# Where the gate projections stand in the state space stage, and when small matmuls of B and C are issued

## The chip, the cores and the metric

The kernel runs on one core of a Trainium2 chip. Five engines work side by side on that core and meet through semaphores: TensorE (PE, the matmuls), VectorE (DVE), ScalarE (ACT), GpSimd (POOL) and SyncE (SP), which here only issues transfers between the chip's memory and the on-chip buffers. The metric is the device time of one execution in microseconds (us). Lower is better.

## What is computed

Two layers of an encoder over 512 tokens of 1024 channels, all in float32. Each layer projects its input once into three branches: a bidirectional state space branch (SSD), differential attention, and cross-attention into 256 memory tokens. Sigmoid gates merge the three, an output projection and a layer norm close the layer. The change lies in the SSD branch and in the gates. Cut to that:

```python
proj = jnp.einsum('bsd,de->bse', x, w_in[layer])
z, xbc, dt_raw, dq, dk, dv, dg, cq, cg, gl = jnp.split(proj, splits, axis=-1)
xbc = jax.nn.silu(_centred_dwconv(xbc, conv_w, conv_b))       # x (32 heads of 64), B and C (4 groups of 128)
# one direction of the chunked scan: 4 chunks of 128 tokens, 4 groups of 8 heads
a_cum = jnp.cumsum(a, axis=-1)
seg = a_cum[..., :, None] - a_cum[..., None, :]
decay = jnp.exp(jnp.where(lower, seg, -jnp.inf))
y_diag = jnp.einsum('bcqgn,bcsgn,bgrcqs,bcsgrp->bcqgrp', cm, bm, decay, xs)
decay_states = jnp.exp(a_cum[..., -1:] - a_cum)
states = jnp.einsum('bcqgn,bgrcq,bcqgrp->bcgrpn', bm, decay_states, xs)
# prev: the states carried from chunk to chunk
y_off = jnp.einsum('bcqgn,bcgrpn,bgrcq->bcqgrp', cm, prev, jnp.exp(a_cum))
# both directions are summed, then
y = y.reshape(Bsz, L, SSD_INNER) * jax.nn.silu(z.astype(jnp.float32))
y_ssd = _rmsnorm(y, norm_w)
gates = jax.nn.sigmoid(gl.reshape(Bsz, S, N_BRANCH, D_MODEL) + gate_b[layer])
merged = gates[:, :, 0] * (y_ssd @ w_br_ssd) + gates[:, :, 1] * (...) + gates[:, :, 2] * (...)
```

## The kernel before

**Units.** Almost all of TensorE's work comes in units: one tile of 128x1024 weights is loaded (`wr`), ScalarE rounds it to `wh`, VectorE computes the rest `wl`, and TensorE makes 24 matmuls of 128x512 from the three products wl*xh, wh*xl, wh*xh into one bank `pj`. Such a unit is called a whole unit below, and its 24 matmuls wide ones. `emit` walks a list of steps, `self.plan`, filled by `self.T(fn, unit)`: a step with a unit gets its weights, loaded and split some steps ahead.

**The SSD stage** (`ssd`) runs once per layer, over 4 groups g of 8 heads. In each group come the units B (`bpart`), C (`cpart`), X0 to X3 (`xpart`: the projection of 128 channels of x, then a convolution on ScalarE and VectorE, `conv`), with the output units W of the group before between them, and in the first group the small DT unit and its tables (`dt_tables`) after X0. Then come `states`, and four times a unit Z (`zpart`) and a block Y (`ypart`). In the trace's names: `bC` and `cC` are B and C after their convolution, `bT` is B transposed on TensorE through the bank `pt`; `gs` is the product of B and C, which `cpart` makes in a bank `pm`; `xsC` is a block of x and `xsT` its transposition; `cum` are the cumulative sums of the decay, which go through ScalarE (`eb`) to the chip's memory (`dab`) and come back, spread over 128 partitions, as `ab`.

**States.** `states` multiplies `xsT` with weights into `xw` on VectorE, and TensorE multiplies `xw` with `bT`, six times: these small matmuls read `xw,bT` in the trace. Every `xw` reads all four blocks of `xsT`.

**Blocks.** `ypart(g, b)` handles two heads. For each it loads `ab` (two buffers, `bufs=2`), takes the minimum with a mask and later the sum and the product with `gs` on VectorE, with eight exponentials on ScalarE between; the product is `m` (three buffers). The eight small matmuls `m,xsT` of the block need both heads' `m`. A new `ab` is loaded when a buffer comes free, which is when the `m` of an earlier head is done.

**Gates.** `AHEAD` says after which block of which group the projection of which gate is made in advance: `(0, 1): [(2, 0)]` puts the gate of branch 2, tile 0, after block (0, 1). Such a unit (`gate_ahead`) is a whole unit whose tanh, `tg`, is stored to memory (`dgt`) and read back later. Nothing near it needs its result, so it is TensorE work that can stand in any place. GATE20 below is the unit of gate (2, 0), and so on.

**Order.** The tile framework has a scheduler that arranges each engine's instructions from the program's order and priorities; on the chip every engine then takes its list in that fixed order. `self.late(n)` lowers the priority of what stands in it by n, so that the scheduler lets work that comes later in the program go first:

```python
    def late(self, n):

        return self.tc.high_priority(offset=-n)
```

`xpart` uses it for its transpositions with LX = 70, `bpart` and `cpart` don't. At the end of the stage, `norm` sums the squares `sqa` (gathered on GpSimd) with four tiny matmuls and makes the scale `rB`, which `fin` needs; `gpart` are the gates of this branch itself, G00 to G07 below.

Of the kernel before, what the change touches and what calls it, by code (L numbers as in the profile page):

```python
# [20 lines left out]
P = 128  # L21
# [15 lines left out]

AHEAD = {(0, 1): [(2, 0)], (0, 2): [(2, 1)], (0, 3): [(2, 2)], (1, 0): [(2, 3)], (1, 2): [(2, 4)],  # L40
         (2, 0): [(2, 5)], (2, 2): [(2, 6)], (3, 0): [(2, 7)], (3, 2): [(1, 0)]}

LX, LD, LN = 70, 80, 300
# [6 lines left out]
def bc(ap, shape):  # L52
    return ap.broadcast_to(shape)


class Net:
# [367 lines left out]
    def ssd(self, l):  # L424
# [10 lines left out]
        def bpart(g):  # L435
            def f(wh, wl):
                self.bC = self.t(self.sp, [P, S], "bC")
                self.conv(self.proj(wh, wl), 16 + g, self.bC)
                pt = self.bank(self.pt, "pt")
                for c in range(4):  # L440
                    self.tr(pt[:, c * P:(c + 1) * P], self.bC[:, c * P:(c + 1) * P])
                self.bT = self.t(self.sp, [P, S], "bT")
                self.act(self.bT, pt)
            return f

        def cpart(g):
            def f(wh, wl):
                self.cC = self.t(self.sp, [P, S], "cC", bufs=2)
                self.conv(self.proj(wh, wl), 20 + g, self.cC)
                pg = self.bank(self.pm, "pm")  # L450
                for c in range(4):
                    q = slice(c * P, (c + 1) * P)
                    self.mm(pg[:, q], self.bC[:, q], self.cC[:, q])
                self.gs = self.t(self.sp, [P, 4, P], "gs", bufs=2)
                self.act(self.gs, pg.rearrange("p (c q) -> p c q", c=4))
                self.xsT = self.t(self.sp, [P, 4, S], "xsT", bufs=2)
                self.xsC = {}
            return f

        def xpart(g, b):  # L460
            def f(wh, wl):
                xc = self.xsC[b] = self.t(self.sp, [P, S], f"xsC{b}")
                self.conv(self.proj(wh, wl), 4 * g + b, xc)
                pt = self.bank(self.pt, "pt")
                with self.late(LX):
                    for c in range(4):
                        self.tr(pt[:, c * P:(c + 1) * P], xc[:, c * P:(c + 1) * P])
                self.act(self.xsT[:, :, b * P:(b + 1) * P], pt.rearrange("p (c e) -> p c e", c=4))
            return f

        def states(g):
            def f():
                sp = self.sp
                self.prev = {}
                for d, order in ((0, (0, 1, 2)), (1, (3, 2, 1))):
                    hs = slice(d * 32 + g * 8, d * 32 + g * 8 + 8)
                    old = None
                    for c in order:
                        xw = self.t(sp, [P, 8, 64], "xw", bufs=2)
                        self.tt(xw, self.xsT[:, c, :].rearrange("p (h e) -> p h e", h=8),  # L480
                                bc(self.wst[:, c, hs, None], [P, 8, 64]), ALU.mult)
                        ps = self.bank(self.pm, "pm")
                        self.mm(ps, self.bT[:, c * P:(c + 1) * P], xw)
                        pv = self.t(sp, [P, 8, 64], f"prev{d}{c}")
                        psv = ps.rearrange("p (h e) -> p h e", h=8)
                        if old is None:
                            self.act(pv, psv)
                        else:
                            self.tt(pv, old, bc(self.dtot[:, c, hs, None], [P, 8, 64]), ALU.mult)
                            self.tt(pv, pv, psv, ALU.add)  # L490
                        old = pv
                        self.prev[d, c + 1 if d == 0 else c - 1] = pv.rearrange("p h e -> p (h e)")
            return f

        def zpart(g, b):
            def f(wh, wl):
                ps = self.proj(wh, wl)
                th = self.t(self.sp, [P, S], "th", bufs=2)
                self.act(th, ps, AF.Tanh, scale=0.5)
                self.sz = self.t(self.sp, [P, S], "sz", bufs=2)  # L500
                self.stt(self.sz, th, 1.0, ps, ALU.add, ALU.mult)
            return f
# [58 lines left out]
        def wpart(g, u):  # L561
            def f(wh, wl):
                yh, yl = self.yhl[g]
                for i in range(2):
                    ps = self.bank(self.pj, "pj")
                    for k in range(4):
                        c = slice(k * 256 + i * P, k * 256 + (i + 1) * P)
                        self.mm3(ps, wh[:, c], wl[:, c], yh[:, k, :], yl[:, k, :], k == 0, k == 3)
                    o = self.br[:, 2 * u + i, :]
                    if g == 0:  # L570
                        self.act(o, ps)
                    else:
                        self.tt(o, o, ps, ALU.add)
            return f

        def keep(g):
            def f():
                self.yhl = {g: (self.yh, self.yl)}
            return f
# [16 lines left out]
        def gpart(j):  # L596
            def f(wh, wl):
                self.gt[j] = self.gate(self.sp, wh, wl, 0, j, "th" if j % 4 < 2 else "sz")
            return f
# [11 lines left out]

        ahead = AHEAD
        self.ahead_gates = {ij for v in ahead.values() for ij in v}
        self.dgt = {}
        self.T(begin)
        for g in range(4):
            jobs = [(bpart(g), (l, UB + g)), (cpart(g), (l, UC + g))]
            jobs += [(xpart(g, b), (l, UXS + 4 * g + b)) for b in range(4)]
            for i, (fn, u) in enumerate(jobs):
                self.T(fn, u)  # L620
                if g == 0 and i == 2:
                    self.T(lambda: self.dt_tables(l))
                if g and i > 1:
                    self.T(wpart(g - 1, i - 2), (l, UBS + 4 * (g - 1) + i - 2))
            self.T(states(g))
            for b in range(4):
                self.T(zpart(g, b), (l, UZ + 4 * g + b))
                self.T(ypart(g, b))
                for i, j in ahead.get((g, b), ()):
                    self.gate_ahead(l, i, j, lambda: self.sp, "tg")  # L630
            self.T(keep(g))
        self.gt = {}
        self.T(norm)
        for j in range(3):
            self.T(gpart(j), (l, UGL + j))
        for u in range(4):
            self.T(wpart(3, u), (l, UBS + 12 + u))
        for j in range(KC):
# [596 lines left out]
```

## Time and profile before

| | |
|---|---|
| time, median of 3 runs | 2219.3 us (2218.12 to 2221.23) |
| the profiled execution's own time | 2223.68 us |
| its span in the trace | 2221.9 us, granted clock 0.997 |
| TensorE busy | 2171.0 us, 98% |
| VectorE busy | 1585.9 us, 71% |
| ScalarE busy | 1004.3 us, 45% |
| SSD stage, layer 0 | from the start to some 470 us |
| SSD stage, layer 1 | some 1162 to 1625 us |

TensorE is busy nearly always, so the time is that of its matmuls and of the few places where it waits. A wait shows as idle time before an instruction, with the engine and the tile that ended it. Since matmuls are pipelined, a wait is read as what the distance of two starts has over its usual value.

### The profile page before, as it was taken

What the parts mean: (1) busy time and instruction counts of PE and PEld (TensorE: products, weight loads), DVE (VectorE), ACT (ScalarE), POOL (GpSimd) and SP (SyncE); (2) the same over time, 40 slices, a digit from 0 to 9 for tenths busy, and PEclk for the clock granted to TensorE, in tenths of its full rate; (3) what the DMA queues carried; (4) which work ended last, traced back from release to release, by engine and by line L of the source; (5) the groups of instructions that cost most, each with busy time, mean ns of one, the idle gap of its engine ahead of it and who ended that gap; (6) DMA issues with size and microseconds to landing.
All of it is one profiled execution on the core that took longest, in us unless ns stands there. A gap on an engine that the chain in (4) does not pass through costs nothing.

```text
span 2221.9 us, 29523 instructions
## 1 busy us (share of the span) xinstructions
PE 2171.0 (98%) x11330; PEld 1768.0 (80%) x11330; DVE 1585.9 (71%) x2440; ACT 1004.3 (45%) x1895; POOL 54.2 (2%) x38
## 2 busy tenths in 40 slices
PE   8999999999999999999999999999999999999998
PEld 6787877788887888878887777777788887888786
DVE  7887878758554777766467888888754547777567
ACT  5664545424442454543355564545423324554440
POOL 0000000000000000000000100000100000000000
PEclk9999999999999999999999999999999999999999
DMA  4654554425553322224564654454434333222353
GB/s 149 182 160 144 144 136 144 125 86 167 168 173 117 95 85 79 77 89 147 152 214 122 177 146 145 133 152 132 124 105 132 105 113 94 75 84 81 91 154 112
DMA packets 106162, 283.73 MB, mean 128 GB/s; under 512 B 12524, under 2 KB 13092, under 8 KB 105764
## 3 DMA queue, kind: packets, MB, share of 16 engines
q1 hardware_dynamic: 106020, 281.84, 42.4%
q8 instruction: 89, 1.46, 0.3%
q14 instruction: 53, 0.43, 0.1%
HBM read 255.55 MB, written 17.85 MB: 123 GB/s over the span
## 4 chain that ended last, share of the span: by engine, by line
PE 71%; DVE 14%; DMA 8%; ACT 5%; issue 1%; POOL 0%; SPq 0%; POOLq 0%; DVEq 0%; ACTq 0%
PE pj L103 55%; PE pm L103 13%; DMA ab<-dab 5%; DVE wl L81 3%; PE pt L111 2%; DVE ab L81 2%; DVE acc L84 2%; ACT ab L91 1%; ACT wh L91 1%; DMA wr<-wu 1%; DVE y L81 1%; DVE rx L81 1%; PE pt L103 1%; DMA fth<-rd 1%; DVE m L81 1%
## 5 line engine op out<-in xcount | busy, mean ns | idle before, releaser
L103 PE MATMUL pj<-xh,wl 128*128 128x512 f32 x1664 | 669.2, 402 | 11.0 <-DVE wl L81 8.9
L103 PE MATMUL pj<-xh,wh 128*128 128x512 f32 x1664 | 661.0, 397 | 0.0
L103 PE MATMUL pj<-xl,wh 128*128 128x512 f32 x1664 | 658.5, 396 | 0.0
L81 DVE TENSOR_TENSOR wl<-wr,wh 128x1024 fp32r<-128x1024 f32 x330 | 405.7, 1230 | 109.0 <-ACT wh L91 108.1
L91 ACT ACTIVATE wh<-wr 128x1024 fp32r<-128x1024 f32 x330 | 347.4, 1053 | 228.4 <-PE pj L103 147.4
L103 PEld LDWEIGHTS pj<-xh,wl 128*128 128x128 f32 x1664 | 313.9, 189 | 91.2 <-issue 18.3
L103 PEld LDWEIGHTS pj<-xh,wh 128*128 128x128 f32 x1664 | 313.8, 189 | 71.7 <-issue 5.7
L103 PEld LDWEIGHTS pj<-xl,wh 128*128 128x128 f32 x1664 | 314.2, 189 | 63.6 <-issue 3.6
L91 ACT ACTIVATE ab<-ab,bias 128x128 f32<-128x128 f32 x512 | 160.8, 391 | 120.5 <-DVE ab L81 119.7
L84 DVE SCALAR_TENSOR_TENSOR acc<-pj,hcw,acc 128x510 f32<-128x510 f32 x192 | 142.4, 744 | 24.2 <-ACT acc L91 22.8
L91 ACT ACTIVATE fpp<-pm,fmx 128x512 f32<-128x512 f32 x128 | 87.9, 687 | 84.3 <-DVE fmx L889 83.6
L889 DVE TENSOR_REDUCE fmx<-pm 128x1 f32<-128x512 f32 x128 | 87.0, 686 | 45.9 <-PE pm L103 45.5
L103 PE MATMUL pj<-yl,wh 128*128 128x512 f32 x256 | 102.4, 400 | 0.9 <-DVE yl L84 0.9
L103 PE MATMUL pj<-yh,wh 128*128 128x512 f32 x256 | 103.0, 403 | 0.0
L81 DVE TENSOR_TENSOR ab<-ab,cst 128x1024 f32<-128x1024 f32 x64 | 85.4, 1334 | 24.4 <-DMA ab<-dab 24.4
L103 PE MATMUL pj<-dy,wh 128*128 128x512 f32 (+1 forms) x384 | 102.2, 354 | 0.1
L103 PE MATMUL pj<-yh,wl 128*128 128x512 f32 x256 | 102.0, 399 | 0.0
L103 PE MATMUL pj<-cy,wh 128*128 128x512 f32 x256 | 78.8, 389 | 0.0
L103 PEld LDWEIGHTS pj<-dy,wh 128*128 128x128 f32 x384 | 67.8, 189 | 11.0 <-DVE dy L81 0.9
L103 PE MATMUL pj<-wh,xl 128*128 128x256 f32 x256 | 74.8, 292 | 0.0
L81 POOL TENSOR_TENSOR sqa<-sqa,sz 128x512 f32<-128x512 f32 x32 | 52.9, 1654 | 845.6 <-ACT sz L91 845.6
L103 PE MATMUL pj<-wl,xh 128*128 128x256 f32 x256 | 72.4, 283 | 0.0
(273 smaller groups left out, 3269.1 us busy)
## 6 DMA issues: line engine op xcount, KB each, us to landing
wr<-wu SPq DMA_DIRECT2D x336, 512.0 KB, 3.7
ab<-dab SPq DMA_DIRECT2D x64, 512.0 KB, 5.7
eb<-deb SPq DMA_DIRECT2D x64, 256.0 KB, 4.7
mkv<-dkv SPq DMA_DIRECT2D x16, 512.0 KB, 4.5
rsw<-rx SPq DMA_DIRECT2D x128, 64.0 KB, 2.0
dgt<-tg SPq DMA_DIRECT2D x18, 256.0 KB, 2.8
dkv<-mo SPq DMA_DIRECT2D x16, 256.0 KB, 4.2
dkv<-q SPq DMA_DIRECT2D x16, 256.0 KB, 3.6
```

Source lines behind the costliest of these rows:

```text
L81: (eng or self.nc.vector).tensor_tensor(out=out, in0=a, in1=b, op=op)
L84: self.nc.vector.scalar_tensor_tensor(out=out, in0=a, scalar=s, in1=b, op0=op0, op1=op1)
L91: self.nc.scalar.activation(out=out, in_=a, func=f, **kw)
L103: self.nc.tensor.matmul(out=out, lhsT=a, rhs=b, start=first, stop=last)
L111: self.nc.tensor.transpose(out=out, in_=x, identity=self.ident)
L889: nc.vector.tensor_reduce(out=mx[:, c:c + 1], in_=ps, axis=AX.X, op=ALU.min)
```

## The change

Three things change, all in the SSD stage. First, `AHEAD` gets a new place, (0, -1), before the states of the first group, and the gates (2, 0) to (2, 4) now stand there and after each of the four blocks of the first group; in the groups 1 and 3 one gate stands after block 1 where one or two stood after the blocks 0 and 2. The same nine gates are made ahead. Second, the transpositions of B and the products of B and C are made in `late(LX)`. Third, the step `norm` is planned after the unit G00 where it was before it.

```diff
-AHEAD = {(0, 1): [(2, 0)], (0, 2): [(2, 1)], (0, 3): [(2, 2)], (1, 0): [(2, 3)], (1, 2): [(2, 4)],
-         (2, 0): [(2, 5)], (2, 2): [(2, 6)], (3, 0): [(2, 7)], (3, 2): [(1, 0)]}
+
+AHEAD = {(0, -1): [(2, 0)], (0, 0): [(2, 1)], (0, 1): [(2, 2)], (0, 2): [(2, 3)], (0, 3): [(2, 4)], (1, 1): [(2, 5)],
+         (2, 0): [(2, 6)], (2, 2): [(2, 7)], (3, 1): [(1, 0)]}
...
                 pt = self.bank(self.pt, "pt")
-                for c in range(4):
-                    self.tr(pt[:, c * P:(c + 1) * P], self.bC[:, c * P:(c + 1) * P])
+                with self.late(LX):
+                    for c in range(4):
+                        self.tr(pt[:, c * P:(c + 1) * P], self.bC[:, c * P:(c + 1) * P])
...
                 pg = self.bank(self.pm, "pm")
-                for c in range(4):
-                    q = slice(c * P, (c + 1) * P)
-                    self.mm(pg[:, q], self.bC[:, q], self.cC[:, q])
+                with self.late(LX):
+                    for c in range(4):
+                        q = slice(c * P, (c + 1) * P)
+                        self.mm(pg[:, q], self.bC[:, q], self.cC[:, q])
...
+            for i, j in ahead.get((g, -1), ()):
+                self.gate_ahead(l, i, j, lambda: self.sp, "tg")
             self.T(states(g))
...
-        self.T(norm)
         for j in range(3):
             self.T(gpart(j), (l, UGL + j))
+            if j == 0:
+                self.T(norm)
```

What the scheduler makes of it is read from the lists of each engine's instructions. Of TensorE, before, here is the place in layer 0, group 0, where B is transposed: `pj_243` is the unit X0, `pj_291` the unit DT that follows it, `pt_180<-cst_81,bC_145` the four transpositions.

```order
L103 MATMUL pj_194<-xh_82,wh_123 128x512
L103 MATMUL pj_243<-xh_82,wl_142 128x512
L103 MATMUL pj_243<-xl_83,wh_141 128x512
L103 MATMUL pj_243<-xh_82,wh_141 128x512
L103 MATMUL pj_243<-xh_82,wl_142 128x512
L103 MATMUL pj_243<-xl_83,wh_141 128x512
L103 MATMUL pj_243<-xh_82,wh_141 128x512
L103 MATMUL pj_243<-xh_82,wl_142 128x512
L111 MATMUL pt_180<-cst_81,bC_145 128x128 x4
```

And of the change, the same four transpositions:

```order
L104 MATMUL pj_243<-xl_83,wh_141 128x512
L104 MATMUL pj_243<-xh_82,wh_141 128x512
L112 MATMUL pt_180<-cst_81,bC_145 128x128 x4
L104 MATMUL pj_291<-xh_82,yl_284 64x512
L104 MATMUL pj_291<-xl_83,yl_284 64x512
```

They stood after the seventh of X0's 24 matmuls and stand after the last. In layer 1 they moved from the 11th to the 24th, in the groups 2 and 3 of both layers from the 15th, in group 1 from the 19th and the 22nd; the products `pm<-cC,bC`, which stood inside the unit after X0, stand after it or inside the next unit, X1.

Of VectorE, before, the place of the first group's states in layer 0: the unit Z0 is evaluated (`sz_112`), then come the states' first products, and behind them the first `ab`.

```order
L84 SCALAR_TENSOR_TENSOR xsC3_84_474<-th_87_501,acc_86_500 128x512
L84 SCALAR_TENSOR_TENSOR sz_112_588<-th_111_586,pj_110_561 128x512
L81 TENSOR_TENSOR wl_126_657<-wr_124_654,wh_125_656 128x1024
L81 TENSOR_TENSOR xw_89_515<-xsT_41_235,wst_57_343 128x512
L81 TENSOR_TENSOR xw_92_521<-xsT_41_235,wst_57_343 128x512
L81 TENSOR_TENSOR ab_119_606<-ab_119_606,cst_4_81 128x1024
```

The same place of the change, on VectorE:

```order
L85 SCALAR_TENSOR_TENSOR xsC3_84_474<-th_87_501,acc_86_500 128x512
L82 TENSOR_TENSOR wl_115_593<-wr_113_590,wh_114_592 128x1024
L82 TENSOR_TENSOR ab_125_641<-ab_125_641,cst_4_81 128x1024
L82 TENSOR_TENSOR xw_95_550<-xsT_41_235,wst_57_343 128x512
L82 TENSOR_TENSOR xw_98_556<-xsT_41_235,wst_57_343 128x512
L85 SCALAR_TENSOR_TENSOR sz_118_623<-th_117_621,pj_116_596 128x512
```

And on ScalarE, of the change, where `pj_521` is GATE20, `pj_596` is Z0 and `pt_509` holds the last block of x, transposed:

```order
L92 ACTIVATE tg_546<-pj_521,hgb_129 128x512
L92 ACTIVATE xsT_235<-pt_462 128x4x128
L92 ACTIVATE wh_592<-wr_590 128x1024
L92 ACTIVATE ab_641<-ab_641,bias_358 128x128 x2
L92 ACTIVATE xsT_235<-pt_509 128x4x128
L92 ACTIVATE ab_641<-ab_641,bias_358 128x128 x3
```

The first `ab` now stands ahead of the first `xw` on VectorE in both layers (before, in layer 1 alone), and two of its exponentials stand ahead of the last block of `xsT` on ScalarE (before, all eight stood behind it).

Of TensorE around the sums of `norm`, in layer 0, before: `pj_3914` is the unit G02.

```order
L103 MATMUL pj_3914<-xh_82,wh_3844 128x512
L103 MATMUL pj_3914<-xh_82,wl_3845 128x512
L103 MATMUL pt_3813<-cst_81,sqa_137 128x1 x4
L103 MATMUL pj_3914<-xl_83,wh_3844 128x512
L103 MATMUL pj_3914<-xh_82,wh_3844 128x512
```

The same place of the change:

```order
L104 MATMUL pj_3914<-xh_82,wh_3815 128x512
L104 MATMUL pj_3914<-xh_82,wl_3816 128x512
L104 MATMUL pt_3846<-cst_81,sqa_137 128x1 x4
L104 MATMUL pj_3914<-xl_83,wh_3815 128x512
L104 MATMUL pj_3914<-xh_82,wh_3815 128x512
```

The four matmuls stand after the 16th of G02's 24 in both, and in layer 1 likewise.

In the first group, TensorE's list now holds two whole units, a gate and a Z, between the blocks 0 and 1 and between 1 and 2, and 52 wide matmuls between 2 and 3 (a gate, the next group's B and four of its C). Before, layer 0 held 35, 38 and 45 there, and layer 1 37, 48 and 54. On VectorE the convolution of the next group's B stood ahead of the last block's second `m` in layer 1, and stands behind it in both layers now. Between the states' first matmul and the first block there are 47 wide matmuls (before, 46 in layer 1). From the transposition of `cum` (`pt<-cst,cum`) to the states' first matmul there are 42 wide matmuls, where there were 30 in layer 0 and 36 in layer 1, and the same small ones but for one pair of `cum`'s matmuls that may stand on either side. In the groups 1 and 3 two units stand between the blocks 0 and 1 and one between 1 and 2, where it was one and then two.

## Rows read from the trace of the kernel before

**Rows 1.** The page, section 1: engine, busy us (share), instructions.

```profile
PE 2171.0 (98%) x11330; PEld 1768.0 (80%) x11330; DVE 1585.9 (71%) x2440; ACT 1004.3 (45%) x1895; POOL 54.2 (2%) x38
```

**Rows 2.** PE's waits, whole span: what was waited for, us, times, longest.

```profile
PE pm L103 <- DVE m L81: 8.2, 8, 2.3
PE pt L111 <- DVE bC L84: 3.6, 4, 1.8
...
PE pt L103 <- POOL sqa L81: 2.4, 2, 1.2
PE pm L103 <- DVE xw L81: 2.3, 2, 1.3
...
PE pm L103 <- DVE cC L84: 0.4, 1, 0.4
```

**Rows 3.** PE's waits between 60 and 115 us (layer 0, first group).

```profile
PE pm L103 <- DVE m L81: 2.8, 3, 1.3
```

**Rows 4.** PE's waits between 1210 and 1285 us (layer 1, first group).

```profile
PE pm L103 <- DVE m L81: 4.2, 3, 2.3
```

**Rows 5.** Timeline, PE: starts of blocks (start us, duration, instruction, [idle <-releaser]).

```profile
84.61 1.09 PE L103 MATMUL pm<-m,xsT 128*64 128x128 f32 x16 [1.27 <-DVE m L81]
96.25 1.09 PE L103 MATMUL pm<-m,xsT 128*64 128x128 f32 x16 [1.03 <-DVE m L81]
...
202.53 1.09 PE L103 MATMUL pm<-m,xsT 128*64 128x128 f32 x16
216.00 1.09 PE L103 MATMUL pm<-m,xsT 128*64 128x128 f32 x16
...
1280.90 1.09 PE L103 MATMUL pm<-m,xsT 128*64 128x128 f32 x16 [2.33 <-DVE m L81]
```

**Rows 6.** Timeline, layer 1, from the transposition of cum to the states.

```profile
1208.17 0.60 PE L111 MATMUL pt<-cst,cum 128*64 128x128 f32 x4
...
1211.83 0.38 SPq L530 DMA_DIRECT2D ab<-dab  x1
...
1216.96 0.60 ACT L91 ACTIVATE xsT<-pt 128x512 f32<-128x512 f32 x1 [0.98 <-PE pt L111]
...
1217.46 0.39 PE L103 MATMUL pj<-xh,wl 128*128 128x512 f32 x1
...
1217.69 0.39 PE L103 MATMUL pj<-xl,wh 128*128 128x512 f32 x1
...
1217.96 1.23 DVE L81 TENSOR_TENSOR ab<-ab,cst 128x1024 f32<-128x1024 f32 x1 [1.15 <-DMA ab<-dab]
...
1219.10 1.29 DVE L81 TENSOR_TENSOR xw<-xsT,wst 128x512 f32<-128x512 f32 x2
1219.22 1.28 ACT L91 ACTIVATE ab<-ab,bias 128x128 f32<-128x128 f32 x4 [0.95 <-DVE ab L81]
...
1219.84 0.70 PE L103 MATMUL pm<-xw,bT 128*128 128x512 f32 x1 [1.06 <-DVE xw L81]
```

**Rows 7.** Timeline, layer 0, the same stretch.

```profile
54.45 0.60 PE L111 MATMUL pt<-cst,cum 128*64 128x128 f32 x4
...
63.45 1.95 PE L103 MATMUL pm<-xw,bT 128*128 128x512 f32 x4
...
65.59 1.23 DVE L81 TENSOR_TENSOR ab<-ab,cst 128x1024 f32<-128x1024 f32 x1 [1.62 <-DMA ab<-dab]
```

**Rows 8.** Transfers that read or write dab, whole span: issue to landing.

```profile
DMA to landing us min/median/max: 3.1/5.6/11.9
```

**Rows 9.** Timeline, layer 1, the load ahead of the first block's second m.

```profile
1230.57 0.37 SPq L530 DMA_DIRECT2D ab<-dab  x1
...
1235.73 1.22 DVE L81 TENSOR_TENSOR ab<-ab,cst 128x1024 f32<-128x1024 f32 x1 [1.30 <-DMA ab<-dab]
```

**Rows 10.** Slice around the sums of layer 0: busy of PE, PEld, DVE, ACT, POOL; clock, DMA share, GB/s.

```profile
440.00:460.00 20.00, 18.79 (x95) 15.09 (x94) 11.11 (x25) 9.46 (x18) 3.06 (x2) 0.91 0.27 79
```

**Rows 11.** Timeline, PE, layer 1, the longest wait for ScalarE (group 1).

```profile
1326.35 0.50 PE L103 MATMUL pj<-xh,wl 128*128 128x512 f32 x1 [1.64 <-ACT mrg L91]
```

## The prediction

> **What bounds the kernel now.** I read the busy shares first: TensorE works 2171.0 of 2221.9 us [rows 1], so some 50 us of waits are all that a change of order can touch, and only those that stand in this stage. The list of what TensorE waited for comes next [rows 2]. The reader should see five entries that belong to the SSD stage: 8.2 us for the blocks' products `m`, 3.6 for `bC`, 2.4 for the squares `sqa`, 2.3 for the states' `xw`, 0.4 for `cC`. The same list cut to the first groups says where: 2.8 us for `m` in layer 0 and 4.2 in layer 1 [rows 3, 4], 7.0 of the 8.2. The rest, 1.2, lies in group 2 of layer 0. Last I read the timeline at each place, for what the wait hangs on.
>
> **Transpositions of B, products with C.** TensorE waits there for VectorE's convolution. The order moves the transpositions behind X0's last matmul. The steady spacing of wide matmuls is 0.23 us (1217.46 to 1217.69, [rows 6]). The longest wait, 1.8, is the one of layer 1's first group, which moves by 13 matmuls, 3.0 us; the waits of groups 2 and 3 (three of the four, 1.8 together) move by 9, 2.1 us, more than any of them is long. Who reads them has time: `bT` is needed by the states alone, five units later. The products move by a unit's end, against a wait of 0.4. So **-4.0 us**. Its bounds are -4.0 and -2.2, if the longest wait shifted with its cause.
>
> **Blocks of the first group.** While TensorE waits for every block, the starts of blocks show VectorE's pace with its loads and exponentials: 84.61 to 96.25, 11.6 us a block [rows 5]. Two whole units between blocks make 13.5 us on TensorE, as 202.53 to 216.00 shows, which had them without a wait [rows 5]. With 48, 48 and 52 wide matmuls TensorE thus comes some 1.8 us or more after the products, at three blocks in each layer. The 2.33 us ahead of layer 1's last block [rows 5] are not of that kind: 54 matmuls stood there already. There B's convolution stood in VectorE's list ahead of the `m`; it stands behind now, so I count that wait as gone too, with less trust. The first block is different, since it hangs on the states. Its second `m` needs a second load that is issued when the first `m` frees a buffer: issue at 1230.57, minimum at 1235.73 [rows 9], and the sum and product after it. All of that follows the first `xw`, and TensorE's distance from the states to this block grows by one matmul only, 0.2 us. The waits there were 1.27 [rows 5] and, in layer 1, the 4.2 less 2.33 and 0.7, some 1.2. VectorE's list holds one product less on this way (0.7 us), so I leave 0.4 of wait in each layer. **-7.0 + 0.8 = -6.2 us**, between -7.0 and -3.5 (the 2.33 stays, and the first blocks keep half of theirs).
>
> **States of the first group.** Here something is late next. With a gate ahead of the states, TensorE arrives later, but the first `ab`, which must come back from memory, now stands ahead of `xw` on VectorE, and two of its exponentials ahead of the last `xsT` on ScalarE. In layer 1 (before) the transposition of `cum` starts at 1208.17 and the minimum at 1217.96, 9.8 us later, of which 6.1 are the load [rows 6]; in layer 0 it is 54.45 to 65.59, 11.1 us [rows 7]. From the minimum's start: 1.26 to the first exponential, 2 x 0.32, 0.60 for `xsT`, 1.29/2 for `xw`, some 0.1 between [rows 6], 3.2 us. So the states' operand is there 13.0 or 14.3 us after the transposition of `cum`. TensorE took 1219.84 - 1208.17 - 1.06 = 10.6 us for that way with 36 wide matmuls [rows 6], and 9.0 with 30 [rows 7]; with 42 it takes 12.0 or 11.8. The wait is 1.0 in layer 1 and 2.5 in layer 0. To this I add a little: the transposition of `cum` itself moves up among the matmuls, while ScalarE's way to `dab` does not shorten by as much. I take 2.1 in each layer, 4.2 for both, in place of 2.3: **+1.9 us**. If `ab` came in 3.1 us, the shortest transfer of `dab` [rows 8], nothing would wait: -2.3. If it took 11.9, the longest [rows 8], each layer would wait 5.8 more: +13.5.
>
> The minimum at VectorE's head is a wait for a transfer in front of work that doesn't need it; behind it stand all six `xw`. The Trainium skill ("DMA: Bandwidth & Descriptors", Rules for kernel authors) says to issue a transfer early, compute, and wait on its semaphore late, which the new list does the other way round. The trace agrees that such a wait costs: 1.15 us of idle VectorE ahead of the minimum, and 1.06 of TensorE right behind it [rows 6]. The Trainium skill's fit for one transfer (the same page, Anatomy of one DMA, made on GpSimd's path) gives 2.0 us and the bytes at 436 GB/s, an estimate of 3.2 us for 512 KB; by that the states would not wait and the sum would be some 4 us lower, but the trace has 6.1 for this load, and that decides.
>
> **Groups 1 and 3.** They hold the same units in another sequence: 13.5 us from block 0 to 1 and 8.0 from 1 to 2, where it was the reverse. The four waits that VectorE's evaluation of block 1 can cause, now 5.4 us later among the products of block 2 and 3, I put at 0 to 1 us each, from blocks that in these groups came without wait [rows 5]; I take 0.2: **+0.8 us**. ScalarE's wait in layer 1 [rows 11] hangs on exponentials standing ahead of the eviction `mrg`; these still do, so 0, from -1.6 to +3.
>
> **Norm, gates, DMA issues.** The sums of the squares stand behind the same 16th matmul, so 2 x 1.2 us stay [rows 2], and so does the clock after them, 0.91 in that slice [rows 10], a part of it at the lower level of 1.2 GHz. Zero. The nine gates, their stores and their weights are as many as before; SP's list gets GATE20's store between the first two `ab` loads, but its tanh is ready before the second buffer's load was issued so far. Zero.
>
> **Sum.** -4.0 - 6.2 + 1.9 + 0.8 = -7.5 us, on the profiled execution's 2223.7, which is 4.4 over the median of the runs. From the median: 2219.3 - 7.5 = **2211.8**. What a measurement can tell from no change here is 0.2%, 4.4 us.
>
> **Rivals.**
> *The first load is no hurdle.* ScalarE and SP reach `dab` sooner, since the sums of `cum` are spread earlier among the matmuls. The states then don't wait (-2.3 in place of +1.9) and the first blocks neither (-0.8): -12.5, 2206.8. For it speaks the lone load, with no weights right ahead of it in SP's list; against it the 9.8 and 11.1 us in both layers. The Trainium skill's fit for a transfer ("DMA: Bandwidth & Descriptors", Anatomy of one DMA) leads to this same case.
> *The waits move on.* The last blocks keep their 2.3, loads of `ab` ahead of `mrg` cost 3 us in group 1, the rest as above: -7.5 + 2.3 + 3 = -2.2, 2217, not to be told from no change. For it speaks that VectorE's list is full of waits for loads of this very kind ([rows 9], and 1.64 us behind ScalarE in [rows 11]).
> *Slower: the first load is slow.* At the head of VectorE's list it holds everything in the stage. At 11.9 us [rows 8] in both layers the sum is -7.5 + 11.6 = +4.1; if the second load, which stands behind it in SP's list, is late with it, the first block's wait is back at its 1.2 (+1.6): +5.7, 2225.0. It decides from a load of some 12 us on. The median of 5.6 [rows 8] speaks against it.
>
> **Chances.** My forecast with its neighbourhood (2208 to 2214.5) 0.50; the first load no hurdle 0.20; the waits move on 0.24; slower 0.06. Faster by more than 4.4 us is below 2214.9: the first two and a small part of the third, 0.72. Same: 0.22. Slower: 0.06. The range takes the bounds of states and blocks on the low side (2205) and most of the third case on the high one (2218).
>
> **What would show each step.** Right: no idle time ahead of `pt<-cst,bC`; no wait for `m` in the first groups but for some tenths at block 0; a wait for `xw` of 1 to 3 us in each layer, with VectorE idle for `ab<-dab` right ahead of the first `xw`; `sqa` at 2.4, 2 times. The forecast is wrong high if the wait for `xw` is gone, wrong low if `mrg`, `wl` or `m` of groups 1 and 3 grow by over 4 us.

## The result: 9.5 us slower, and the profile after

The changed kernel takes 2228.27 us (median, 2225.81 to 2232.84), the kernel before 2218.71 us beside it (2216.73 to 2221.23): ratio 1.0043, 95% interval 1.003 to 1.0056. A ratio is turned into microseconds with 2217 here and below, so the change costs 9.5 us (6.7 to 12.4). By the intervals of the runs, a difference between two such ratios is known to some 3.5 us either way. 2211.8 was forecast, with 2218 as the upper end: the prediction was wrong, in sign too. The profiled execution of the changed kernel took 2228.46 us, its span is 2226.7. The two traces lie only 4.8 us apart, since the execution of [rows 1] was above its kernel's median and this one is not; so the waits below are read one by one, and not as a sum that must give 9.5.

The page's first section, kernel after (as in [rows 1]):

```profile
PE 2174.3 (98%) x11330; PEld 1772.2 (80%) x11330; DVE 1588.5 (71%) x2440; ACT 1005.1 (45%) x1895; POOL 54.4 (2%) x38
```

The work is the same: the instructions are as many, VectorE's busy time differs by 2.6 us, TensorE's by 3.3, part of it matmuls at the lower clock (last section). What changed is when TensorE waits.

PE's waits over the whole span, of the kernel after (as in [rows 2]: what was waited for, us, times, longest):

```profile
PE pj L104 <- DVE acc L85: 6.6, 4, 2.0
PE pm L104 <- DVE m L82: 4.6, 3, 1.9
PE pm L104 <- DVE xw L82: 3.7, 2, 2.8
...
PE pt L104 <- POOL sqa L82: 2.4, 2, 1.2
...
PE pt L112 <- DVE bC L85: 1.9, 2, 1.3
```

Much that was forecast is there: `m` fell from 8.2 to 4.6 and none of it is left in the first groups, `xw` is at 3.7 (4.2 forecast), `sqa` is unchanged, `cC` is gone. What was not forecast is the first row. `acc` is the accumulator of the convolutions; the wait stands in the units W0.0 and W1.0 (the first output unit of groups 0 and 1, made among B and C of the next group), whose second half needs the bank `pj` that VectorE's convolution of C has yet to read. And `bC`, which `late` should have ended, keeps 1.9.

The same places on TensorE's timeline, kernel after (start us, duration, instruction, [idle <-releaser]):

```profile
140.57 0.66 PE L112 MATMUL pt<-cst,bC 128*128 128x128 f32 x4 [0.63 <-DVE bC L85]
146.03 0.50 PE L104 MATMUL pj<-yh,wl 128*128 128x512 f32 x1 [2.04 <-DVE acc L85]
...
249.34 0.50 PE L104 MATMUL pj<-yh,wl 128*128 128x512 f32 x1 [1.24 <-DVE acc L85]
...
427.75 1.09 PE L104 MATMUL pm<-m,xsT 128*64 128x128 f32 x16
435.79 1.09 PE L104 MATMUL pm<-m,xsT 128*64 128x128 f32 x16
449.90 1.09 PE L104 MATMUL pm<-m,xsT 128*64 128x128 f32 x16 [1.93 <-DVE m L82]
```

**End of group 0.** What VectorE did before those waits, kernel after (its timeline, layer 0; the first two rows are the states of group 0):

```profile
64.97 1.23 DVE L82 TENSOR_TENSOR ab<-ab,cst 128x1024 f32<-128x1024 f32 x1 [2.77 <-DMA ab<-dab]
67.44 1.29 DVE L82 TENSOR_TENSOR xw<-xsT,wst 128x512 f32<-128x512 f32 x2 [1.24 <-ACT xsT L92]
...
129.72 0.75 DVE L85 SCALAR_TENSOR_TENSOR acc<-pj,hcw,acc 128x510 f32<-128x510 f32 x1 [1.22 <-ACT acc L92]
132.72 1.23 DVE L82 TENSOR_TENSOR ab<-ab,cst 128x1024 f32<-128x1024 f32 x1 [2.26 <-DMA ab<-dab]
...
139.84 0.68 DVE L85 SCALAR_TENSOR_TENSOR bC<-th,acc 128x512 f32<-128x512 f32 x1
...
143.93 2.71 DVE L85 SCALAR_TENSOR_TENSOR acc<-pj,hcw,acc 128x511 f32<-128x511 f32 x4
```

And the kernel before, same engine, same work:

```profile
126.22 0.68 DVE L84 SCALAR_TENSOR_TENSOR bC<-th,acc 128x512 f32<-128x512 f32 x1
...
132.82 0.68 DVE L84 SCALAR_TENSOR_TENSOR cC<-th,acc 128x512 f32<-128x512 f32 x1
...
134.09 1.21 DVE L81 TENSOR_TENSOR ab<-ab,cst 128x1024 f32<-128x1024 f32 x1
...
135.88 1.22 DVE L81 TENSOR_TENSOR ab<-ab,cst 128x1024 f32<-128x1024 f32 x1
```

The minimum at 132.72 is the layer's tenth and belongs to the second head of group 1's first block, whose products TensorE reads at 202.5, some 70 us later. In the new list it stands after the first of four steps of B's convolution, and VectorE idles 2.26 us for its load with the rest of the convolution, the last block's sums and C's convolution behind it. Before, both minima of that block (134.09 and 135.88) stood behind `cC`, their loads had landed, and nothing waited.

**Ends of groups 1 and 3.** Busy time by stretch (us, PE, PEld, DVE, ACT, POOL busy, clock, DMA share, GB/s), 433 to 450 us, which holds the last blocks of group 3; first the kernel after, then before:

```profile
433.00:450.00 17.00, 15.07 (x85) 12.18 (x85) 16.97 (x23) 10.34 (x24) 2.92 (x2) 1.00 0.34 100
```

```profile
433.00:450.00 17.00, 17.00 (x104) 13.79 (x103) 13.40 (x20) 8.54 (x18) 1.29 (x1) 1.00 0.39 125
```

With one unit between blocks 1 and 2 (8.0 us, 427.75 to 435.79) VectorE has two blocks to evaluate in a row and works 16.97 of 17.0 us; the last `m` comes 1.93 late. With the second gap at 13.5 us it had 3.6 us to spare. The three gaps between the blocks of group 3 one by one, kernel after:

```profile
414.27:427.75 13.48, 13.48 (x77) 11.12 (x76) 8.67 (x13) 4.42 (x6) 2.13 (x1) 1.00 0.53 126
427.75:435.79 8.04, 8.04 (x54) 6.63 (x53) 5.84 (x11) 4.67 (x12) 0.00 (x0) 1.00 0.43 165
435.79:449.90 14.11, 12.18 (x72) 10.03 (x71) 14.08 (x18) 9.55 (x23) 2.92 (x2) 1.00 0.38 111
```

VectorE (the third busy time) works 8.67 of 13.48 us in the long gap and 5.84 of 8.04 in the short one. Most of its idle time in these two is for ScalarE (`th`, `wh`) and for an `ab` load. The work that is left comes in the last gap, where it is busy 14.08 of 14.11 us. Before, the same three gaps held 6.81 of 8.03, 11.74 of 13.48 and 10.45 of 12.11 us.

### The profile page after: what moved, and what is told of

Its sections match the earlier page's. It is cut to its first block, busy times and chain, and to the rows that moved or that the text cites. A ratio compares the mean times of both kernels' runs of the same rounds, so it can differ in the third digit from the quotient of the medians.

```text
span 2226.7 us, 29508 instructions
## 1 busy us (share of the span) xinstructions
PE 2174.3 (98%) x11330; PEld 1772.2 (80%) x11330; DVE 1588.5 (71%) x2440; ACT 1005.1 (45%) x1895; POOL 54.4 (2%) x38
## 4 chain that ended last, share of the span: by engine, by line
PE 71%; DVE 17%; DMA 6%; ACT 4%; issue 2%; SPq 0%; POOLq 0%; DVEq 0%; POOL 0%; ACTq 0%
PE pj L104 56%; PE pm L104 13%; DVE wl L82 3%; DMA ab<-dab 3%; PE pt L112 2%; DVE ab L82 2%; DVE acc L85 2%; DVE y L82 2%; ACT wh L92 1%; DVE eb L82 1%; DVE rx L82 1%; PE pt L104 1%; DVE y L85 1%; ACT ab L92 1%; DMA wr<-wu 1%
```

## The experiments

The theory from these rows: two things cost, the minimum at VectorE's head at the end of group 0, and the crowded ends of groups 1 and 3; `late` and the gates of group 0 are gains. The rivals: `late` itself is to blame (it moved the transpositions and all that follows), or VectorE simply has too much work wherever the gates are put early. All have five rounds but for the norm, which has three.

**The parts alone.** First `late(LX)` alone on the kernel before, around the transpositions of B and, likewise, the products with C:

```diff
+                with self.late(LX):
                     for c in range(4):
                         self.tr(pt[:, c * P:(c + 1) * P], self.bC[:, c * P:(c + 1) * P])
```

> The kernel before with the transpositions of B and the products of B and C in late(LX), and nothing else of the change. Theory V (VectorE's head: the new places of the gates put minimum operations that wait for ab loads ahead of the convolution of the next group's B and C, and crowd VectorE at the ends of the groups 1 and 3; late() is innocent): the waits for bC and cC, 4.0 us, go or shrink, and nothing new of over 1 us comes: 2 to 4 us under the kernel before, about 2215 to 2217. Theory L (late() delays bT and gs and with them what follows, and shifts VectorE's list; the gates are a gain): 5 to 9 us over the kernel before, about 2224 to 2228, with waits for acc of some 6 us.

2212.71 us, ratio 0.998 (0.9971 to 0.999): -4.4 us, a little more than expected. PE's waits:

```profile
PE pm L103 <- DVE m L81: 6.1, 6, 1.7
...
PE pm L103 <- DVE xw L81: 0.7, 1, 0.7
```

`bC`, `cC` and `mrg` are gone from the list. `late` is not to blame by itself. Next the new `AHEAD` alone, with the two lines that serve its place ahead of the states:

```diff
+            for i, j in ahead.get((g, -1), ()):
+                self.gate_ahead(l, i, j, lambda: self.sp, "tg")
```

> The kernel before with the new table of gates alone. Theory V: the waits for m of the first group (7.0 us) go, but waits for acc in group 1 and 2 and for m at the last block of group 3 (some 2 us in each layer) stay as in the changed kernel: 4 to 12 us over the kernel before, about 2223 to 2231. Theory L: 5 to 7 us under the kernel before, about 2212.

2224.66 us, ratio 1.0032 (1.002 to 1.0045): +7.1 us. Its PE waits, and then its VectorE:

```profile
PE pm L103 <- DVE m L81: 7.1, 5, 2.5
...
PE pj L103 <- DVE acc L84: 2.5, 2, 1.2
...
PE pj L103 <- ACT mrg L91: 2.1, 2, 1.6
```

```profile
136.05 0.69 DVE L84 SCALAR_TENSOR_TENSOR bC<-th,acc 128x512 f32<-128x512 f32 x1
...
140.81 1.21 DVE L81 TENSOR_TENSOR ab<-ab,cst 128x1024 f32<-128x1024 f32 x1
```

Here the minimum still stands behind `bC`, without a wait, and the `acc` waits are those of group 1's end alone. Of the 7.1 us for `m`, 3.3 lie in the first groups, where none was expected. So with this table it takes `late` as well to put the minimum ahead of B's convolution. Then the step `norm` behind G00 alone:

```diff
-        self.T(norm)
         for j in range(3):
             self.T(gpart(j), (l, UGL + j))
+            if j == 0:
+                self.T(norm)
```

> The kernel before with the step norm planned after G00, and nothing else. Every engine's list is the same as before's, row by row, but for the numbers in the names. All theories: no difference (within 2 us of the kernel before), sqa 1.2 us twice; the trace is a second look at the kernel before, and shows which of its waits recur.

2218.25 us, ratio 1.0001 (0.9992 to 1.001): nothing, as forecast.

**Groups 1 and 3.** All of the change but `norm`, with the gates of groups 1 and 3 behind block 2:

```diff
-AHEAD = {(0, -1): [(2, 0)], (0, 0): [(2, 1)], (0, 1): [(2, 2)], (0, 2): [(2, 3)], (0, 3): [(2, 4)], (1, 1): [(2, 5)],
-         (2, 0): [(2, 6)], (2, 2): [(2, 7)], (3, 1): [(1, 0)]}
+AHEAD = {(0, -1): [(2, 0)], (0, 0): [(2, 1)], (0, 1): [(2, 2)], (0, 2): [(2, 3)], (0, 3): [(2, 4)],
+         (1, 2): [(2, 5)], (2, 0): [(2, 6)], (2, 2): [(2, 7)], (3, 2): [(1, 0)]}
```

> late() and the five gates of the first group as in the change, but the gates of the groups 1 and 3 behind block 2 in place of block 1 (two units then stand between the blocks 2 and 3 ahead, and between 1 and 2, as in the kernel before); norm as before. Theory V: the waits for m at the last blocks of the groups 1 and 3 (4.6 us) and for acc in group 2 (2.5 us, with the lower clock behind them some 3 more) go, those of group 1 (acc 4.1, bC 1.9) stay: 7 to 10 us under the changed kernel, about 2218 to 2221. Theory L: not more than 4.6 under the changed kernel, 2224 to 2228, with the acc waits of both groups.

2217.8 us, ratio 1.0000 (0.9991 to 1.0009): 9.5 us better than the change, for two numbers in a table (and `norm`, which is worth nothing). No wait for `m` is left at all; `acc` has 4.1 in two places, the ends of group 0. The converse, `late` and the old table with one gate in each of groups 1 and 3 moved from behind block 2 to behind block 1:

```diff
-AHEAD = {(0, 1): [(2, 0)], (0, 2): [(2, 1)], (0, 3): [(2, 2)], (1, 0): [(2, 3)], (1, 2): [(2, 4)],
-         (2, 0): [(2, 5)], (2, 2): [(2, 6)], (3, 0): [(2, 7)], (3, 2): [(1, 0)]}
+AHEAD = {(0, 1): [(2, 0)], (0, 2): [(2, 1)], (0, 3): [(2, 2)], (1, 0): [(2, 3)], (1, 1): [(2, 4)],
+         (2, 0): [(2, 5)], (2, 2): [(2, 6)], (3, 0): [(2, 7)], (3, 1): [(1, 0)]}
```

> late() and the table of gates of the kernel before, but in the groups 1 and 3 the gate behind block 2 moved behind block 1, as the change has it; group 0 as before. The prediction put this part at +0.8 us. Theory V (the crowded end of the groups): the waits of the changed kernel come in groups 1 to 3 and in no other place, m at the last block of group 3 (some 2 us in each layer) and of group 1 (0 to 0.8), acc in group 2 (1.2 in each layer): against the run of late() alone, 2212.7, 6 to 9 us more, 2218.5 to 2221.5. If these waits come from the first group's five gates instead (VectorE enters group 1 late), 2212 to 2214.

2223.68 us, ratio 1.0029 (1.0019 to 1.004): +6.4, so 10.8 worse than `late` alone and above the 2218.5 to 2221.5 expected. Its waits for `acc` are back (2.5, 2 times), and waits for `m` at the ends of groups 1 and 3. Of its 13.8 us for `m`, 9.7 lie in group 0, where the list is the same as with `late` alone (6.1 there), so of the 10.8 the waits of groups 1 and 3 in this one trace (4.1 for `m`, 2.5 for `acc`) show 6.6.

**The minimum.** The change, with this one minimum held back: its input gets zero times a column of `cC` added (`self.zero` makes that column), so it can't stand ahead of C's convolution. Cut to the lines that do it:

```diff
+                    if g == 1 and b == 0 and hh == 1:
+                        z = self.zero(self.cC[:, 0:1])
+                        self.tt(ab[:, 0, 0, 0:1], ab[:, 0, 0, 0:1], z, ALU.add)
```

> The changed kernel, with one minimum held back: the second head's of the first block of group 1 now also reads the finished cC (a number of cC times zero is added to one column of ab), so that VectorE's list has it behind the convolutions of B and C; two tiny operations more in each layer. All loads are issued as before. Theory V (that minimum waits for its load at the head of VectorE's list, with the convolutions of B and C behind it): the waits for acc in group 1 (2 x 2.05) and for bC there (0.6 and 1.3) go, and with them the lower clock behind them in layer 1 (some 1.7): about 2220 to 2222, 6 to 8 under the changed kernel. Theory B (a backlog: VectorE simply has too much to do at the end of the first group, since the gates have moved its blocks together; where the minimum stands doesn't matter): 0 to 2 under the changed kernel.

2217.92 us, ratio 1.0002 (0.9993 to 1.0012): 9.1 us back, at the price of two tiny instructions in each layer, and more than expected. TensorE's list is unchanged, but on VectorE a few instructions around the minimum moved with it, and on SyncE one load of weights changed places with others, so not all loads are issued as before. `bC` is gone, of `acc` 2.5 are left, in group 1's end. Both repairs together, on the kernel with the gates of groups 1 and 3 behind block 2:

> The kernel of the run with the gates of the groups 1 and 3 behind block 2, and the same minimum held back. Theory V: 2217.8 less acc (4.1) and bC (1.5), about 2212, the same as late() alone. Theory B: 2216 to 2218.

2209.69 us (2206.84 to 2213.24), ratio 0.9963 (0.9951 to 0.9976): -8.2 us, better than both kernels and, with a later run of 2209.97, the best here. The lists moved by the hold as in the run above. Its PE waits, and its busy times in the last gap of group 3, between the same two blocks as the third of the rows above:

```profile
PE pm L103 <- DVE xw L81: 2.6, 2, 1.6
...
PE pt L103 <- POOL sqa L81: 2.4, 2, 1.2
...
PE pj L103 <- DVE acc L84: 0.3, 1, 0.3
```

```profile
428.30:440.41 12.11, 12.11 (x71) 10.00 (x70) 10.16 (x15) 6.65 (x14) 1.29 (x1) 1.00 0.34 118
```

VectorE works 10.16 of 12.11 us here, and TensorE doesn't wait for the block.

**The gate ahead of the states.** Two tables without it, since it is what makes the states wait, both with `late` and with `norm` as before. First with four gates in group 0 and two in group 3, the minimum held:

```diff
+AHEAD = {(0, 0): [(2, 0)], (0, 1): [(2, 1)], (0, 2): [(2, 2)], (0, 3): [(2, 3)], (1, 2): [(2, 4)],
+         (2, 0): [(2, 5)], (2, 2): [(2, 6)], (3, 0): [(2, 7)], (3, 2): [(1, 0)]}
```

> late(), gates behind each of the four blocks of group 0 and none ahead of the states (VectorE's list then has two xw ahead of the first minimum), gates of the other groups behind (1, 2), (2, 0), (2, 2), (3, 0), (3, 2), and the minimum of group 1 held back. Theory V: no acc or bC waits; xw under 1 us; the first block of group 0 waits some 1 us as in the kernel before; 2209 to 2212. If the gate ahead of the states were what frees the blocks, 2213 to 2216, with waits for m of over 4 us.

2215.21 us, ratio 0.9988 (0.998 to 0.9997): -2.7, where 2209 to 2212 was expected. `xw` falls to 0.4, but `acc` takes 3.8, at the two ends of group 0, with no minimum in the way: with one whole unit less in group 0 VectorE works from 123.99 to 139 without a pause and reaches C's convolution late all the same. The rival of too much work is a part of the truth. VectorE's stretch (third busy time), and then TensorE's wait:

```profile
123.99:139.00 15.01, 13.04 (x60) 10.27 (x59) 14.94 (x20) 8.72 (x14) 2.13 (x1) 1.00 0.56 163
```

```profile
137.02 0.50 PE L103 MATMUL pj<-yh,wl 128*128 128x512 f32 x1 [1.97 <-DVE acc L84]
```

Then two gates behind block 3, nothing held:

```diff
+AHEAD = {(0, 0): [(2, 0)], (0, 1): [(2, 1)], (0, 2): [(2, 2)], (0, 3): [(2, 3), (2, 4)], (1, 2): [(2, 5)],
+         (2, 0): [(2, 6)], (2, 2): [(2, 7)], (3, 2): [(1, 0)]}
```

> late(), no gate ahead of the states, one gate behind each of the blocks 0 to 2 of group 0 and two behind block 3, one each behind (1, 2), (2, 0), (2, 2), (3, 2); nothing held back. VectorE's list has two xw ahead of the first minimum, and the minimum of group 1 stands ahead of all of B's convolution with one split (wl) between, not among its parts; TensorE has two units between the last block and B. Theory V: xw under 1 us, no acc and bC waits of over 1 us, some 1 us for the first block: 2207 to 2210, the fastest or as fast as the fastest so far. If the first group's five gates crowd VectorE wherever its minimum stands: acc waits of 1.9 as in the run with no gate ahead of the states, 2213 to 2216.

2219.52 us, ratio 1.0006 (0.9997 to 1.0015): the expectation of 2207 to 2210 missed by 10 us. VectorE, and then TensorE:

```profile
127.79 1.22 DVE L81 TENSOR_TENSOR ab<-ab,cst 128x1024 f32<-128x1024 f32 x1 [5.02 <-DMA ab<-dab]
...
140.15 0.69 DVE L84 SCALAR_TENSOR_TENSOR bC<-th,acc 128x512 f32<-128x512 f32 x1
```

```profile
140.90 1.12 PE L111 MATMUL pt<-cst,bC 128*128 128x128 f32 x4 [3.47 <-DVE bC L84]
```

The same minimum again, now ahead of all of B's convolution, with an idle time of 5.02 us. This gave the cleanest test: the same kernel with the minimum held by the three lines shown above. TensorE's and SyncE's lists stay the same. The expectation is not quite right that every other instruction keeps its place: the minimum takes its sum and, on ScalarE, its eight exponentials along, and the first head's sum and one `yl` move up by a few places.

> As the run with gates behind blocks 0 to 3 and none ahead of the states, but for one thing: the minimum of group 1's first block, second head, is held behind C's convolution; every other instruction keeps its place in its list. In the run without the hold this minimum stood at VectorE's head 5.0 us for its load, in front of the last block's sums and of B's convolution, and TensorE then waited 3.5 and 3.3 us for bC. If the waiting minimum is the cause, both bC waits go, the load is hidden, and the time falls by 6 to 9 us from 2219.5: 2210.5 to 2213.5, ratio 0.997. If VectorE simply has too much work there in this order (as where no gate stood ahead of the states, which kept 1.9 us of acc in each layer with the same minimum held), some 2 us a layer stay as waits for bC or acc: 2214 to 2217, ratio 0.998 to 0.9995. If the minimum has nothing to do with it: 2219.5.

2209.97 us, ratio 0.9967 (0.9954 to 0.998): 8.7 us less (by the ratios), for one instruction, with what hangs on it, in another place. VectorE, and then TensorE, in the same stretch:

```profile
124.55 1.23 DVE L81 TENSOR_TENSOR wl<-wr,wh 128x1024 fp32r<-128x1024 f32 x1 [2.08 <-ACT wh L91]
...
135.80 0.69 DVE L84 SCALAR_TENSOR_TENSOR bC<-th,acc 128x512 f32<-128x512 f32 x1
...
144.51 1.23 DVE L81 TENSOR_TENSOR ab<-ab,cst 128x1024 f32<-128x1024 f32 x1
```

```profile
136.89 0.60 PE L116 MATMUL pt<-cst,bC 128*128 128x128 f32 x4
```

`bC` is 4.35 us earlier, and TensorE doesn't wait. The idle time for the load is not all of that: VectorE idles 2.08 us at the same place without it, for `wh`, so the load adds 2.9. The minimum and its sum, 1.22 and 0.68 us long, stand ahead of `bC` only without the hold. So the pair shows what the place of this minimum costs, and not how that splits between the wait and the work in front.

**The first minimum.** Last, the kernel of 2209.69 with the very first minimum held too, behind the second `xw`, against the 2.6 us of `xw`:

```diff
+                    if g == 0 and b == 0 and hh == 0:
+                        z = self.zero(self.xw[1][:, 0, 0:1])
```

> As the run before, and the first head's minimum of the first block of group 0 held behind the states' second xw as well (VectorE's list then has it behind all six). Theory V: the waits for xw (3.6 in that kernel's trace) go down to less than 1 and 2 to 3 us come off against the run before, about 2209 to 2210. Rival: the first block's second m is late by what the minimum was put back, and TensorE waits 2 to 4 us there in place of the states: no gain, 2211 to 2213.

2220.58 us, ratio 1.0014 (1.0002 to 1.0026), 11.3 us worse, where a gain was expected. PE's waits:

```profile
PE pj L103 <- DVE acc L84: 5.4, 2, 2.7
PE pm L103 <- ACT prev L91: 3.9, 2, 2.6
PE pm L103 <- DVE m L81: 3.7, 4, 1.8
```

`xw` is gone, but the scheduler answered with other pairs of minima in all of group 0 and put a minimum ahead of B's convolution again (the first head's this time, at 133.80, idle 3.03 for its load). And TensorE waits for the states' `prev` instead. ScalarE, in the stretch of that wait in layer 0:

```profile
72.90 1.06 ACT L91 ACTIVATE wh<-wr 128x1024 fp32r<-128x1024 f32 x1 [6.06 <-DMA wr<-wu]
```

The last `prev` stands behind this `wh`, which waits for its weights. In the run before, the same `wh` waited 3.44 us at 72.53, and TensorE, held up by `xw`, lost only 0.16 us to `prev`. So the wait for `xw` hid another one of the same kind. How the 11.3 us split between the two is not tried.

## Why the prediction was wrong

**Transpositions of B, products with C** (-4.0): -4.4 measured on the kernel before, close in number and in part by luck: the waits for `bC` and `cC`, read at 4.0 us, are only 1.1 and 0.4 in another execution of the same lists (last section). What it left out is that other instructions move too. On the new table `late` gains nothing (+7.1 without it, +9.5 with it, intervals that overlap), since it is then that the minimum goes to the head; with the minimum held the change is 6.7 below the table alone.

**Blocks of the first group** (-6.2) and **States of the first group** (+1.9): together -4.3, and -3.8 measured (the run with both repairs against `late` alone, -8.2 and -4.4; a difference known to some 3.5 either way), but only with the minimum held. Without the hold the same gates cost 4.4. The waits themselves came as forecast: none for `m`, `xw` 2.76 in layer 0 and 0.95 in layer 1 against 2.5 and 1.0 ahead of the small addition, VectorE idle for `ab<-dab` ahead of the first `xw` and ScalarE's `xsT` behind two exponentials. The 0.8 left for the first block wasn't needed. What failed is what the prediction made of the convolution of B that "stands behind now". That the last block's `m` went ahead of it was counted, and that wait did go. That a minimum of the next group went ahead of it too was not, so the sum has no term for it, which puts it at nothing. The price of the missing term: 8.2 (the gates of group 0, held or not), 9.1 (the change), 8.7 (the cleanest pair).

**Groups 1 and 3** (+0.8): +9.5 measured, and +8.6 with the minimum held (1.0002 against 0.9963). This is the step that was mis-sized most. It priced four waits at 0 to 1 us from blocks that came without wait; the trace after has five, of 7.0 us together: 1.24 and 1.23 for `acc`, 1.93, 0.76 and 1.87 for `m`. The rest of the 9.5 is not traced wait by wait; the granted clock fell behind one of them (last section). The mistake was to take the spacing of the blocks as a matter of TensorE's distance only. VectorE's work doesn't shrink with it: in group 3 it is idle 4.8 of 13.5 us in the long gap and 2.2 of 8.0 in the short one, and then works 14.08 of 14.11 us.

**Norm, gates, DMA issues** (0): right for `norm`, which alone gave 1.0001 and whose waits stay at 2.4; the other two weren't tried alone.

The sum by the runs: -4.4 (`late`) - 3.8 (gates of group 0) + 8.2 (the minimum) + 9.5 (groups 1 and 3, with `norm`) = +9.5. These are differences along one path from before to change, so they must close; along another path single terms differ by about 1 us, `late` by more.

Of the rivals, "the waits move on" had the right mechanism, a wait for an `ab` load that stands ahead of work TensorE needs, but put it ahead of `mrg` at 3 us and left out VectorE's lack of slack. "Slower: the first load is slow" had the right sign and the wrong place: the first load cost what was forecast, the tenth, of the next group, did the harm. The rule of the Trainium skill ("DMA: Bandwidth & Descriptors", Rules for kernel authors), to issue early, compute and wait late, was weighed for the first load alone. The runs agree with it more strongly elsewhere: one minimum put behind the work that doesn't need it gave back 8 to 9 us, three times.

The price is more than the waits. In the cleanest pair, bC's waits are 6.8 us together, of 8.7 by the runs. The rows put the rest down to the clock behind them, which no run tries by itself. The same stretch behind the wait, without the hold and then with it (columns as above):

```profile
140.00:146.00 6.00, 5.10 (x14) 4.22 (x15) 5.83 (x9) 3.91 (x6) 0.00 (x0) 0.50 0.26 89
```

```profile
140.00:146.00 6.00, 6.00 (x32) 5.09 (x31) 5.90 (x10) 3.52 (x6) 0.00 (x0) 1.00 0.36 122
```

After an idle time of 3.47 us TensorE was granted the lower level, 1.2 GHz (0.50), and made 14 matmuls in these 6 us, of which it was idle for 0.9, where it made 32 at 2.4 GHz.

What stays open: the table's share of group 0 is -2.4 without `late` (7.1 less 9.5) and +4.4 with it and no hold. That the place of the minimum makes this difference is argued, not tried by a run of the table and the hold without `late`.

## What to carry to other kernels

When a scheduler's order changes, go down the list of each in-order engine and mark every instruction that waits for a transfer; what stands right behind it is what the transfer can delay, even if the instruction itself belongs to work that is due 70 us later. Filling TensorE in front of one block moves the slack of the engine that feeds it too: a long gap in which that engine idles gives it nothing for later, and the gaps behind it must be priced as its busy time against the distance, not as "came without wait". And a part that is a gain alone can be a loss together with another, so each part is tried alone and in the whole.

## What had not been expected of the hardware

Two executions of the same instruction lists differ much in their waits. The run with `norm` moved has the lists of the kernel before but for buffer numbers; its profiled span is 2213.9 us against 2221.9, and its PE waits are these, where [rows 2] has 8.2, 3.6 and 2.3:

```profile
PE pm L103 <- DVE m L81: 5.9, 6, 1.5
...
PE pm L103 <- DVE xw L81: 1.4, 2, 0.7
...
PE pt L111 <- DVE bC L84: 1.1, 3, 0.5
```

The prediction priced its gains from the slower of the two, an execution above the median, and so priced the waits for `bC` and `m` higher than the other has them.

The clock does not fall after every wait. In the kernel after, the `acc` wait of 2.04 us was followed by full speed (first row), that of 1.24 us at 249.34, with another of 0.38 at 247.36 (for `yl`) just ahead of it, by the lower level (second row):

```profile
146.00:152.00 6.00, 5.97 (x30) 5.06 (x31) 5.58 (x8) 3.27 (x5) 0.00 (x0) 1.00 0.29 87
250.00:253.00 3.00, 3.00 (x10) 2.35 (x9) 3.00 (x5) 0.00 (x0) 0.00 (x0) 0.56 0.34 57
```

What decides between them is not settled here.
